# Row-wise infinity norm of an 8192 x 8192 matrix: another order and other cuts of the loads, a split first load, and a last result transposed before it is stored

## The chip, the core and the metric

The kernel runs on one core of one Trainium2 chip. The metric is the device time of one execution in microseconds. Most executions of one kernel agree within 0.3%. The profile shows a single execution and gives times from the start of its span.

## The reference

```python
def setup_inputs():
    return {
       "x": np.random.randn(8192, 8192).astype(np.float32),
    }

def reference(x: np.ndarray) -> np.ndarray:
    return np.linalg.norm(x, ord=np.inf, axis=1)
```

For a matrix given with `axis=1` this is the vector norm of each row: the largest absolute value among its 8192 elements. 8192 rows give 8192 results. The input is 268.4 MB of fp32, the output 32 KB; each element is read once and takes part in one maximum.

## The kernel before

A row of the matrix lies on one partition, so 128 rows of the matrix, one for each partition, make what this text calls a row of the tile grid, or simply a row: 128 partitions by 8192 columns, 4 MB. There are 64 such rows. They are numbered in 32 groups of R = 2 (L47, `x_g` in L53): partition p of group g holds the matrix rows 256 g + 2 p and 256 g + 2 p + 1, one after the other, 16384 columns. What one partition reads in a group is contiguous in HBM.

`_pieces` (L23) cuts this sequence of 64 x 8192 columns into loads. Up to where the tail begins each load is a whole group, 16384 columns. The tail is the list `TAIL` (L14): eight single rows of 8192 columns and then 14 pieces that shrink from 6400 to 1408. A piece that would cross a group's border is cut there. The list comes to 25 groups, 8 single rows and 14 pieces, 47 loads.

All loads go into one buffer, `ring` (L59), of three groups' size, 49,152 columns. A position `at` moves through it and returns to 0 when the next piece does not fit any more (L76). SP issues each load (L81), in order, and waits in front of it for the DVE reduces that read the columns which the load will overwrite. So at most three groups are in the ring, and a load is issued as soon as its part of the ring is free.

DVE takes each piece as it lands, in the same order. A whole row, or two, are reduced in one instruction straight into `res` (L87). A part of a row is reduced into a slot of `part` (L96), and when the row's last part is done a second reduce, the join, takes the maximum over its slots into `res` (L98). `absmax` (L65) is `tensor_reduce` with maximum and absolute value, on fp32.

`res` holds 64 results on each partition. When group 30 is complete, the results of the first 31 groups are transposed on TensorE into PSUM with an identity matrix (L108), copied by ACT to `o_sb` (L109) and stored from ACT's queue in two DMAs of 16 and 15 partitions, with 1 KB a partition (L111, L112). The last group's results, two numbers on each of 128 partitions, are stored directly by SP as 128 runs of 8 bytes (L113). This store waits for the last join.

There is no other order than that of the program on each engine: SP has the loads and the last store, DVE the reduces and joins, ACT the copies and two stores, TensorE two transposes, POOL the identity matrix at the start.

Of the kernel before, what the change touches and what calls it, by code (L numbers as in the profile page):

```python
# [1 line left out]

# [5 lines left out]

P = 128
FP32 = mybir.dt.float32  # L10

TAIL = (  # L14
    [8192] * 8
    + [6400, 5888, 4096]
    + [4992, 4544, 3776, 3072]
    + [3264, 2944, 2624, 2304, 2112, 1728, 1408]
)
RING = 3 * 16384  # L20


def _pieces(total, n_cols, pair):  # L23

    tail = sum(TAIL)
    assert (total - tail) % pair == 0
    cuts = [(a, a + pair) for a in range(0, total - tail, pair)]
    at = total - tail
    for w in TAIL:
        end = at + w  # L30
        while at < end:
            e = min(end, (at // pair + 1) * pair)
            cuts.append((at, e))
            at = e
    return cuts


@with_exitstack
def kernel(
    ctx: ExitStack,  # L40
    tc: tile.TileContext,
    x: bass.AP,
    out: bass.AP,
):
    nc = tc.nc
    n_rows, n_cols = x.shape
    R = 2  # L47
    pair = R * n_cols
    G = n_rows // (P * R)
    total = n_rows // P * n_cols  # L50


    x_g = x.rearrange("(g p r) m -> g p (r m)", p=P, r=R)  # L53
    out_g = out.rearrange("(g p r) -> g p r", p=P, r=R)

    single = ctx.enter_context(tc.tile_pool(name="single", bufs=1))
    psum_pool = ctx.enter_context(tc.tile_pool(name="psum", bufs=1, space=bass.MemoryType.PSUM))

    ring = single.tile([P, RING], FP32)  # L59
    res = single.tile([P, G, R], FP32)  # L60
    part = single.tile([P, G * R, 8], FP32)
    ident = single.tile([P, P], FP32)
    make_identity(nc, ident)

    def absmax(dst, src):  # L65
        nc.vector.tensor_reduce(  # L66
            out=dst, in_=src, axis=mybir.AxisListType.X,
            op=mybir.AluOpType.max, apply_absolute_value=True,
        )

    n_part = {}
    flushed = False
    at = 0
    for a, b in _pieces(total, n_cols, pair):
        w = b - a
        if at + w > RING:  # L76
            at = 0
        g = a // pair
        buf = ring[:, at : at + w]
        at += w  # L80
        nc.sync.dma_start(out=buf, in_=x_g[g, :, a - g * pair : b - g * pair])  # L81
        s = a
        while s < b:
            row = s // n_cols
            if s % n_cols == 0 and b - s >= n_cols:
                k = (b - s) // n_cols
                absmax(  # L87
                    res[:, g, row % R : row % R + k],
                    buf[:, s - a : s - a + k * n_cols].rearrange("p (k m) -> p k m", m=n_cols),
                )  # L90
                s += k * n_cols
                continue
            e = min(b, (row + 1) * n_cols)
            i = n_part.get(row, 0)
            n_part[row] = i + 1
            absmax(part[:, row, i : i + 1], buf[:, s - a : e - a])  # L96
            if e == (row + 1) * n_cols:
                nc.vector.tensor_reduce(  # L98
                    out=res[:, g, row % R : row % R + 1], in_=part[:, row, : i + 1],
                    axis=mybir.AxisListType.X, op=mybir.AluOpType.max,  # L100
                )
            s = e
        if b == (G - 1) * pair and not flushed:
            flushed = True
            o_sb = single.tile([G - 1, P, R], FP32)
            for r in range(R):
                o_ps = psum_pool.tile([G - 1, P], FP32, name=f"o_ps{r}")
                nc.tensor.transpose(o_ps, res[:, : G - 1, r], ident)  # L108
                nc.scalar.copy(o_sb[:, :, r], o_ps)  # L109
            h = (G - 1) // 2 + 1  # L110
            nc.scalar.dma_start(out=out_g[:h], in_=o_sb[:h])  # L111
            nc.scalar.dma_start(out=out_g[h : G - 1], in_=o_sb[h:])  # L112
    nc.sync.dma_start(out=out_g[G - 1], in_=res[:, G - 1, :])  # L113


# [1 line left out]
_INS = ['x']  # L117
_OUTS = [((8192,), 'float32')]


# [23 lines left out]
```

## Time and profile before

| | |
|---|---|
| median of 11 runs | 632.55 us (631.98 to 633.05) |
| the profiled execution | 632.35 us |
| its span | 630.5 us |
| DVE busy | 552.3 us, 88% of the span |
| HBM read | 268.44 MB, a mean of 426 GB/s over the span |
| first load issued, landed | 0.74 us, 22.54 us |
| last DVE wait for a load ends | 564.97 us |
| last join ends | 626.71 us |
| last store issued | 626.73 us, 2.8 us to landing |

The span is the time that the profile covers; the execution's own time is 1.85 us longer. The page divides the span into 40 slices and gives the busy share of each engine in tenths. The chain of waits is followed back from the last instruction: at each step to what released it, or to the instruction before it on the same engine. A time "to landing" counts from the issue of a DMA to its completion, so for loads that are issued early it contains the loads in front of them in the queue.

### The profile page before, as it was taken

To read this page: it belongs to the slowest core of one execution; us is meant where nothing else is said; L and a number is where in the kernel's file an instruction comes from. 1 tells how busy PE (TensorE), PEld (TensorE's weight loads), DVE (VectorE), ACT (ScalarE), POOL (GpSimd) and SP (SyncE) were. 2 spreads that over 40 slices of the span, in tenths; PEclk is the share of its full clock that TensorE was granted. 3 is DMA by queue.
4 is the path that set the end of the run, shared out by engine and by line. 5 is a ranking of instruction groups with operands and counts; after the bars stand their busy time and mean duration, and the time that the engine had idled before them with its cause. 6 is when DMAs were issued, how large, how long until landed. Compare 5 with 4: busy or idle time off the path is not lost.

```text
span 630.5 us, 200 instructions
## 1 busy us (share of the span) xinstructions
PE 0.8 (0%) x2; PEld 0.2 (0%) x2; DVE 552.3 (88%) x56; ACT 1.8 (0%) x3; POOL 0.7 (0%) x6
## 2 busy tenths in 40 slices
PE   0000000000000000000000000000000000000000
PEld 0000000000000000000000000000000000000000
DVE  0588988888988889888899888898888999999997
ACT  0000000000000000000000000000000000000000
POOL 0000000000000000000000000000000000000000
DMA  9999999999999999999999999999999999999995
GB/s 399 420 445 449 416 457 407 428 437 399 466 437 428 457 407 466 399 466 399 466 399 466 399 466 399 466 399 466 399 466 399 432 432 432 432 437 425 420 426 224
DMA packets 6975, 268.48 MB, mean 426 GB/s; under 512 B 927, under 2 KB 958, under 8 KB 1214
## 3 DMA queue, kind: packets, MB, share of 16 engines
q1 hardware_dynamic: 6912, 268.44, 98.8%
q10 hardware_dynamic: 62, 0.03, 0.0%
q14 instruction: 1, 0.01, 0.0%
HBM read 268.44 MB, written 0.03 MB: 426 GB/s over the span
## 4 chain that ended last, share of the span: by engine, by line
DMA 62%; DVE 37%; issue 0%
DMA ring<-in_x_dram 62%; DVE res L66 29%; DVE part L66 8%; DVE res L98 0%
## 5 line engine op out<-in xcount | busy, mean ns | idle before, releaser
L66 DVE TENSOR_REDUCE res<-ring 128x2 f32<-128x16384 f32 (+1 forms) x33 | 499.3, 15149 | 74.3 <-DMA ring<-in_x_dram 74.3
L66 DVE TENSOR_REDUCE part<-ring 128x1 f32<-128x4096 f32 (+15 forms) x17 | 52.7, 3156 | 0.0
L109 ACT COPY o_sb<-o_ps 31x128 f32<-31x128 f32 x2 | 0.5, 263 | 607.1 <-PE o_ps L108 607.1
L108 PE MATMUL o_ps<-ident,res 128*31 128x128 f32 x2 | 0.8, 404 | 608.5 <-DVE res L98 608.5
L109 ACT ACT_TABLE_LOAD x1 | 1.3, 1283 | 0.7 <-PEq L128 0.7
L98 DVE TENSOR_REDUCE res<-part 128x1 f32<-128x2 f32 (+2 forms) x6 | 0.9, 151 | 0.1
L108 PEld LDWEIGHTS o_ps<-ident,res 128*31 128x31 f32 x2 | 0.2, 125 | 608.8 <-issue 601.5
masks.py:199 POOL TENSOR_SCALAR_AFFINE_SELECT ident<-ident 128x128 f32<-128x128 f32 x1 | 0.3, 292 | 0.1
masks.py:197 POOL MEMSET ident<- 128x128 f32 x1 | 0.2, 204 | 0.3 <-POOLq L128 0.3
L128 POOL MEMSET const-bfloat16-1.0<- 128x1 bf16 x1 | 0.1, 101 | 0.0
L128 POOL MEMSET const-uint8-127<- 128x1 uint8 x1 | 0.1, 101 | 0.0
L128 POOL MEMSET const-float32-0.0<- 128x1 f32 x1 | 0.1, 98 | 0.2 <-issue 0.2
L128 POOL MEMSET const-float32-1.0<- 128x1 f32 x1 | 0.1, 98 | 0.0
## 6 DMA issues: line engine op xcount, KB each, us to landing
ring<-in_x_dram SPq DMA_DIRECT2D x8, 4096.0 KB, 40.5
ring<-in_x_dram SPq DMA_DIRECT2D x1, 3200.0 KB, 42.3
ring<-in_x_dram SPq DMA_DIRECT2D x1, 2944.0 KB, 40.7
ring<-in_x_dram SPq DMA_DIRECT2D x1, 2496.0 KB, 42.9
ring<-in_x_dram SPq DMA_DIRECT2D x1, 2272.0 KB, 39.7
ring<-in_x_dram SPq DMA_DIRECT2D x1, 2048.0 KB, 45.2
ring<-in_x_dram SPq DMA_DIRECT2D x1, 1888.0 KB, 44.0
ring<-in_x_dram SPq DMA_DIRECT2D x1, 1632.0 KB, 43.4
```

The source lines that it names most:

```text
L66: nc.vector.tensor_reduce(out=dst, in_=src, axis=mybir.AxisListType.X, op=mybir.AluOpType.max, apply_absolute_value=True,)
L98: nc.vector.tensor_reduce(out=res[:, g, row % R : row % R + 1], in_=part[:, row, : i + 1], axis=mybir.AxisListType.X, op=mybir.AluOpType.max,)
L108: nc.tensor.transpose(o_ps, res[:, : G - 1, r], ident)
L109: nc.scalar.copy(o_sb[:, :, r], o_ps)
L128: nc = _bacc.Bacc("TRN2", target_bir_lowering=False, num_devices=1)
```

## The change

The order and the cuts of the loads are written out in `PIECES`: four single rows first, then 24 pairs as whole loads, four pairs that are cut (into 2, 2, 2 and 3 pieces), three single rows cut into 2, 3 and 4 pieces, and the last row in six pieces from 1792 down to 896. The single rows have the matrix's last 1024 rows, one matrix row on each partition; the pairs have the others, two on each partition as before.

The first load is issued as two DMAs, partitions 0 to 15 and partitions 16 to 127.

Rows from number `CUT` = 48 on go into `part`, which has K = 4 slots for each and is cleared by POOL at the start. One reduce over all slots of 15 rows replaces the joins. It stands after the last but one row, and the stores of the first 63 rows' results follow it: `pairs_out` (two transposes, one store of 28 partitions) and `singles_out` (one transpose, one store of 7 partitions), on TensorE, ACT and ACT's queue.

The last row's first five pieces leave their maxima in five columns behind the buffer of its sixth piece, `last`, which lies outside the ring. The final reduce covers the sixth piece and these columns at once. Its result, one number on each of 128 partitions, is transposed on TensorE, copied from PSUM by DVE and stored by SP from one partition, 512 bytes.

```diff
--- before.py
+++ after.py
@@ -8,31 +8,25 @@
 
 P = 128
 FP32 = mybir.dt.float32
+MAX = mybir.AluOpType.max
 
 
 
-TAIL = (
-    [8192] * 8
-    + [6400, 5888, 4096]
-    + [4992, 4544, 3776, 3072]
-    + [3264, 2944, 2624, 2304, 2112, 1728, 1408]
+
+HEAD = 4
+PAIRS = 28
+PIECES = (
+    [[8192]] * HEAD
+    + [[16384]] * 24
+    + [[7232, 9152], [6720, 9664], [8640, 7744], [5568, 5568, 5248]]
+    + [[4480, 3712], [3392, 1920, 2880], [2752, 1600, 2048, 1792]]
+    + [[1792, 1664, 1472, 1280, 1088, 896]]
 )
 RING = 3 * 16384
 
 
-def _pieces(total, n_cols, pair):
-
-    tail = sum(TAIL)
-    assert (total - tail) % pair == 0
-    cuts = [(a, a + pair) for a in range(0, total - tail, pair)]
-    at = total - tail
-    for w in TAIL:
-        end = at + w
-        while at < end:
-            e = min(end, (at // pair + 1) * pair)
-            cuts.append((at, e))
-            at = e
-    return cuts
+CUT = 48
+K = 4
 
 
 @with_exitstack
@@ -44,73 +38,114 @@
 ):
     nc = tc.nc
     n_rows, n_cols = x.shape
-    R = 2
-    pair = R * n_cols
-    G = n_rows // (P * R)
-    total = n_rows // P * n_cols
+    R = n_rows // P
+    assert R == 64 and n_cols == 8192
 
-
-    x_g = x.rearrange("(g p r) m -> g p (r m)", p=P, r=R)
-    out_g = out.rearrange("(g p r) -> g p r", p=P, r=R)
+    X_ONE = 2 * PAIRS
 
     single = ctx.enter_context(tc.tile_pool(name="single", bufs=1))
     psum_pool = ctx.enter_context(tc.tile_pool(name="psum", bufs=1, space=bass.MemoryType.PSUM))
 
     ring = single.tile([P, RING], FP32)
-    res = single.tile([P, G, R], FP32)
-    part = single.tile([P, G * R, 8], FP32)
+    res = single.tile([P, R - 1], FP32)
+    part = single.tile([P, R - 1 - CUT, K], FP32)
+    nc.gpsimd.memset(part, 0.0)
     ident = single.tile([P, P], FP32)
     make_identity(nc, ident)
 
+
+    n_last = len(PIECES[-1]) - 1
+    w_last = PIECES[-1][-1]
+    last = single.tile([P, w_last + n_last], FP32)
+    fin = single.tile([P, 1], FP32)
+
     def absmax(dst, src):
         nc.vector.tensor_reduce(
-            out=dst, in_=src, axis=mybir.AxisListType.X,
-            op=mybir.AluOpType.max, apply_absolute_value=True,
+            out=dst, in_=src, axis=mybir.AxisListType.X, op=MAX, apply_absolute_value=True,
         )
 
-    n_part = {}
-    flushed = False
+    def singles_out():
+        n = R - 1 - X_ONE
+        ps = psum_pool.tile([n, P], FP32, name="ps_singles")
+        sb = single.tile([n, P], FP32, name="sb_singles")
+        nc.tensor.transpose(ps, res[:, X_ONE:], ident)
+        nc.scalar.copy(sb, ps)
+        nc.scalar.dma_start(
+            out=out[X_ONE * P : (R - 1) * P].rearrange("(r p) -> r p", p=P), in_=sb
+        )
+
+    def pairs_out():
+        sb = single.tile([PAIRS, P, 2], FP32, name="sb_pairs")
+        both = res[:, :X_ONE].rearrange("p (g r) -> p g r", r=2)
+        for r in range(2):
+            ps = psum_pool.tile([PAIRS, P], FP32, name=f"ps_pairs{r}")
+            nc.tensor.transpose(ps, both[:, :, r], ident)
+            nc.scalar.copy(sb[:, :, r], ps)
+        nc.scalar.dma_start(
+            out=out[: X_ONE * P].rearrange("(g p r) -> g p r", p=P, r=2), in_=sb
+        )
+
     at = 0
-    for a, b in _pieces(total, n_cols, pair):
-        w = b - a
-        if at + w > RING:
-            at = 0
-        g = a // pair
-        buf = ring[:, at : at + w]
-        at += w
-        nc.sync.dma_start(out=buf, in_=x_g[g, :, a - g * pair : b - g * pair])
-        s = a
-        while s < b:
-            row = s // n_cols
-            if s % n_cols == 0 and b - s >= n_cols:
-                k = (b - s) // n_cols
-                absmax(
-                    res[:, g, row % R : row % R + k],
-                    buf[:, s - a : s - a + k * n_cols].rearrange("p (k m) -> p k m", m=n_cols),
-                )
-                s += k * n_cols
-                continue
-            e = min(b, (row + 1) * n_cols)
-            i = n_part.get(row, 0)
-            n_part[row] = i + 1
-            absmax(part[:, row, i : i + 1], buf[:, s - a : e - a])
-            if e == (row + 1) * n_cols:
-                nc.vector.tensor_reduce(
-                    out=res[:, g, row % R : row % R + 1], in_=part[:, row, : i + 1],
-                    axis=mybir.AxisListType.X, op=mybir.AluOpType.max,
-                )
-            s = e
-        if b == (G - 1) * pair and not flushed:
-            flushed = True
-            o_sb = single.tile([G - 1, P, R], FP32)
-            for r in range(R):
-                o_ps = psum_pool.tile([G - 1, P], FP32, name=f"o_ps{r}")
-                nc.tensor.transpose(o_ps, res[:, : G - 1, r], ident)
-                nc.scalar.copy(o_sb[:, :, r], o_ps)
-            h = (G - 1) // 2 + 1
-            nc.scalar.dma_start(out=out_g[:h], in_=o_sb[:h])
-            nc.scalar.dma_start(out=out_g[h : G - 1], in_=o_sb[h:])
-    nc.sync.dma_start(out=out_g[G - 1], in_=res[:, G - 1, :])
+    next_pair, next_one = 0, X_ONE
+    for u, widths in enumerate(PIECES):
+        k = sum(widths) // n_cols
+        if k == 2:
+            row, next_pair = next_pair, next_pair + 2
+        else:
+            row, next_one = next_one, next_one + 1
+        src = x[row * P : (row + k) * P].rearrange("(p r) m -> p (r m)", r=k)
+        off = 0
+        n_part = {}
+        for h, w in enumerate(widths):
+            final = u == len(PIECES) - 1 and h == n_last
+            if final:
+                buf = last[:, :w]
+            else:
+                if at + w > RING:
+                    at = 0
+                buf = ring[:, at : at + w]
+                at += w
+            if u == 0:
+                nc.sync.dma_start(out=buf[:16], in_=src[:16, off : off + w])
+                nc.sync.dma_start(out=buf[16:], in_=src[16:, off : off + w])
+            else:
+                nc.sync.dma_start(out=buf, in_=src[:, off : off + w])
+            if final:
+                absmax(fin[:, :1], last)
+                break
+            s = 0
+            while s < w:
+                r = row + (off + s) // n_cols
+                left = n_cols - (off + s) % n_cols
+                c = (w - s) // n_cols if left == n_cols else 0
+                if c and r + c <= CUT:
+                    absmax(
+                        res[:, r : r + c],
+                        buf[:, s : s + c * n_cols].rearrange("p (c m) -> p c m", m=n_cols),
+                    )
+                    s += c * n_cols
+                    continue
+                e = min(w, s + left)
+                i = n_part.get(r, 0)
+                n_part[r] = i + 1
+                if r == R - 1:
+                    absmax(last[:, w_last + i : w_last + i + 1], buf[:, s:e])
+                else:
+                    absmax(part[:, r - CUT, i : i + 1], buf[:, s:e])
+                s = e
+            off += w
+        if u == len(PIECES) - 2:
+            nc.vector.tensor_reduce(
+                out=res[:, CUT:], in_=part, axis=mybir.AxisListType.X, op=MAX,
+            )
+            pairs_out()
+            singles_out()
+
+    fin_ps = psum_pool.tile([1, P], FP32)
+    fin_sb = single.tile([1, P], FP32)
+    nc.tensor.transpose(fin_ps, fin, ident)
+    nc.vector.tensor_copy(out=fin_sb, in_=fin_ps)
+    nc.sync.dma_start(out=out[(R - 1) * P :].rearrange("(r p) -> r p", p=P), in_=fin_sb)
 
 
 # ---- launch: one core; inputs and outputs as the reference has them ----
```

## The prediction, made before the changed kernel had run

> **What bounds the kernel now.** I read the page's shares and 40 slices first, then the chain of waits, then the groups split by shape, the windows of the start, the timeline of the tail and the DMA issues.
>
> ```profile
> PE 0.8 (0%) x2; PEld 0.2 (0%) x2; DVE 552.3 (88%) x56; ACT 1.8 (0%) x3; POOL 0.7 (0%) x6
> DVE  0588988888988889888899888898888999999997
> DMA  9999999999999999999999999999999999999995
> ```
>
> The DMA engines are full from the first slice to the last but one, DVE is near 88% and reaches 9 only in the last ten slices. So the load stream is the bound for most of the span and DVE comes close to it. The chain of waits shows where one hands over to the other:
>
> ```profile
> 0.74 21.80 DMA ring<-in_x_dram
> ...
> 446.49 40.78 DMA ring<-in_x_dram
> 487.27 0.02 issue
> 487.29 34.42 DVE res L66 x3
> 521.71 0.02 issue
> 521.73 43.24 DMA ring<-in_x_dram
> 564.97 0.02 issue
> 564.99 8.69 DVE res L66
> ...
> 618.41 8.12 DVE part L66 x4
> 626.52 0.02 issue
> 626.55 0.16 DVE res L98
> ```
>
> Columns are start, duration, what. Up to 487.27 each step is a load, and 50 of the 64 column rows (a row is 8192 columns on each partition) have landed. The eight single rows that follow land 9.71 us apart ((564.97 - 487.27) / 8). The last wait of DVE for a load ends at 564.97. From there DVE runs without a gap to 626.71: the end is set by DVE, not by the last landing.
>
> ```profile
> L66 DVE TENSOR_REDUCE res<-ring 128x2 f32<-128x16384 f32 x25 | 430.5, 17220 | 74.0 <-DMA ring<-in_x_dram 74.0
> L66 DVE TENSOR_REDUCE res<-ring 128x1 f32<-128x8192 f32 x8 | 68.9, 8677 | 0.3 <-DMA ring<-in_x_dram 0.3
> L66 DVE TENSOR_REDUCE part<-ring 128x1 f32<-128x1408 f32 x1 | 1.6, 1610 | 0.0
> ```
>
> 17220 minus 8677 over 8192 columns is 1.043 ns a column, and what is left is about 0.14 us an instruction, part of which overlaps the instruction before. In the gapless stretch 564.99 to 626.71 there are 57,344 columns in 24 instructions (18 reduces, 6 joins): at 1.0417 ns a column (the slope from 16384 down to 1408 columns) 59.73 us are columns, so 1.99 us, 83 ns for each instruction, are overhead. A load costs 1.18 ns a column (19.35 us between starts of two pair reduces, over 16384). DVE thus gains only 0.14 ns a column on the stream, while at a pair's landing it is 17.22 us behind.
>
> ```profile
> 0.00:22.56 22.56, 0.00 (x0) 0.00 (x0) 0.00 (x0) 1.28 (x1) 0.70 (x6) 1.00 1.00 418
> 22.56:41.91 19.35, 0.00 (x0) 0.00 (x0) 17.22 (x1) 0.00 (x0) 0.00 (x0) 1.00 1.00 434
> ```
>
> The last column of the windows is GB/s. The first pair takes 21.80 us from issue where 19.35 is the steady figure: 2.45 us of start, of which 0.98 us pass before the first packet in the trace's packet records.
>
> ```profile
> 608.90 0.42 PE L108 MATMUL o_ps<-ident,res 128*31 128x128 f32 x1 [6.96 <-DVE res L98]
> 609.36 0.26 ACT L109 COPY o_sb<-o_ps 31x128 f32<-31x128 f32 x1 [7.12 <-PE o_ps L108]
> 609.65 0.38 ACTq L111 DMA_DIRECT2D out_dram<-o_sb  x1
> 626.73 0.35 SPq L113 DMA_DIRECT2D out_dram<-res  x1
> ```
>
> The final store is issued 0.02 us after the last join and lands 2.79 us later (2.8 in the list of issues), at 629.52; the span ends 0.98 us after that. The transpose at 608.90 is the model for the new one.
>
> [...] In the packet records the 8-byte store lands 1.75 us after its last packet, the 1 KB-row stores 0.48 us after theirs[...].
>
> **The change part by part.** The diff is priced as it stands: the last row is transposed on TensorE and stored as one 512 byte run, not on DVE in 128 byte runs as the words of the change have it.
>
> *Order and cuts of the rows.* Four single rows, then 24 pairs, then 12 rows in 24 pieces. SP issues without a stall: the ring still holds 49,152 columns, a slot comes free 17.2 us after its landing, and then 19.35 plus 2.13 us of loads are still queued. In the tail the pieces are small and the ring holds over ten of them. Starting with single rows lets DVE begin some 9.7 us earlier, which is worth nothing, as DVE then waits for loads anyway (2.13 us before each pair, 74.0 in all).
> The tail is worth something. Before, the last pair lands with 14 rows to go, now with 12. Before, 52 rows had landed at 487.27 + 2 x 9.71 = 506.70. Two more singles in place of a pair cost 2 x 0.04 us and the first tile's second DMA about as little: 506.8. From there DVE has the pair, 17.22 us, then 98,304 columns, 102.40 us, in 28 reduces (four pieces cross a row's end) and one join, 29 x 0.083 = 2.41 us; the join over 60 elements and the 5 old partials in the final reduce add 0.06. DVE ends at 506.83 + 17.22 + 102.40 + 2.41 + 0.06 = 628.92, against 626.71: **+2.21 us**. The stream would deliver the last piece near 624.5 (before: 624.33), so DVE is some 3 to 4 us behind it all along the tail, and no piece's landing is waited for. Six joins merged into one and the last row's join folded into its last reduce are in this count.
>
> *The last row's result.* New after the last reduce: semaphore to TensorE 0.04 and transpose 0.42 (row at 608.90), 0.04 to the copy, a copy of 1 x 128 out of PSUM on DVE, then 0.02 to SP. The copy is not in the trace; ACT's is 0.26[...]. Sum 0.78, less the 0.02 of before: **+0.76 us**. Nothing hides it; DVE has nothing else to do.
>
> *The final store.* One 512 byte run in place of 128 of 8 bytes. Upper bound: 2.79 as before. Lower bound: 0.85 to the first packet (626.73 to 627.58), 0.05 of data, 0.48 to landing, 1.38 us. I take 1.6, nearer the lower[...]: **-1.2 us**.
>
> *The other stores* (28 rows of 1 KB, 7 of 512 B) go out on ACT's queue once the merged join is done, about 619.4. Two transposes, copies and an issue, then 5 us to landing under load as before, 626 to 627: hidden behind the last row's reduces. If that cover went, the late part would be 1 or 2 us. The memset of the partials on POOL is done long before the first landing: nothing.
>
> *The first tile in two DMAs.* SP issues once more, 0.33 us, while the queue is full: nothing. [...] The start's own delay (about 1.1 us of 2.45 lie after the first packet) can hide inside it, some 0.7. [...] A tile lands with its slowest engine, and the stream never gets a loss back, since it is full. Bounds -0.3 us [...] and +8.5. I take 3.64 - 0.7 + 1.3 = **+4.2 us**. All of it moves the landing of row 52 and DVE's chain with it.
>
> Sum against the profiled execution: 630.5 + 2.21 + 0.76 - 1.2 + 4.2 = 636.5 span. That execution took 632.35, 1.85 more than its span: 638.3. It lies 0.2 below the median, 632.55, so 638.5.
>
> **The rivals.**
> [...] (first tile costs nothing): 630.5 + 2.21 + 0.76 - 1.2 = 632.3, with 2.05 added 634.3, 0.3% slower. For it: the two DMAs follow each other in one queue and engines might run ahead into the second. [...]
> *Not slower, the start is won.* [...] Price: up to 0.25 us of the 0.98 and 0.7 to 0.8 of the 1.1, near -1.0. [...] that gives 633.3, with the store at its lower bound 633.1, within 0.2% of before. It decides from a start that lands row 52 at 506.1 or sooner. For it: 2.45 us of start are visible. Against: the time to the first packet of the tiny last store is 0.85, hardly less than 0.98.
> *The split is worse than priced*: [...] 8.5 us of start, 642.8.
>
> **How the numbers follow.** [...] as priced 0.50 (about 636.8 to 640.5), worse than priced 0.12[...], start won 0.12. The range leaves out the start won and most of the worst case: 633.5 to 642. A run of this kernel can tell a change from none at about 0.2%, 1.27 us (631.3 to 633.8). Slower: 0.50 + 0.12 + three quarters of 0.26 and a little of the last, 0.83; same 0.13; faster 0.04.
>
> **What would show it.** Right: the last DVE wait for a load ends at the last full pair, and DVE is gapless from there for 122 us; the last piece lands 3 us or more before its reduce starts; the first single lands near 16 us[...]; a PE, a DVE copy and a store shorter than 2 us end the chain. Wrong: DVE waiting for pieces in the tail (then the lag was mis-sized), a first landing below 13 us [...], or a final store again near 2.8 us. The forecast falls as a whole if the first landing and every later one stand where they did; what is left then is the 0.3% of the tail.

## The result: 1.5% slower

The changed kernel takes 641.99 us in the median (641.83 to 642.27, 8 runs), against 632.49 for the kernel before in the same comparison (31 runs). The ratio is 1.0151, with a 95% interval of 1.0142 to 1.0160. The forecast was 638.5 with a range of 633.5 to 642.0: the direction held, and the loss, 9.5 us, was 1.6 times the forecast one, at the very edge of the range.

First the rates, from the page (HBM rate in 40 slices of about 16 us, the kernel before and then the changed one) and from the windows of the changed kernel (the last column is GB/s):

```profile
GB/s 399 420 445 449 416 457 407 428 437 399 466 437 428 457 407 466 399 466 399 466 399 466 399 466 399 466 399 466 399 466 399 432 432 432 432 437 425 420 426 224
GB/s 203 375 434 430 454 418 438 450 401 458 442 409 454 401 454 450 401 458 426 426 454 397 458 450 401 454 413 442 450 401 458 442 394 439 435 427 425 421 422 202
```
```profile
0.00:22.60 22.60, 0.00 (x0) 0.00 (x0) 0.00 (x0) 1.28 (x1) 0.78 (x7) 1.00 0.95 229
22.60:32.20 9.60, 0.00 (x0) 0.00 (x0) 8.69 (x1) 0.00 (x0) 0.00 (x0) 1.00 1.02 437
```

The first slice moves half of what it did before, the second is lower too, the third and later ones run as before. The first tile, 4 MB, lands at 22.60 us, when the kernel before had 8 MB: 229 GB/s in place of 418. Note the next to last column, the share of time in which the DMA engines had a packet: 0.95. They are occupied nearly all the while and move at about half the rate, so the busy share of the DMA engines does not show the loss. From the second tile on (437 GB/s) the rate is as it was.

The chain of waits of the changed kernel (start, duration, what):

```profile
475.23 40.78 DMA ring<-in_x_dram
516.01 0.03 issue
516.04 17.22 DVE res L63
533.26 95.19 DVE part L63 x22
628.45 0.02 issue
628.48 0.22 DVE res L138
...
636.62 1.10 DVE fin L63
637.73 0.04 issue
637.77 0.39 PE fin_ps L146
638.15 0.02 issue
638.18 0.28 DVE fin_sb L147
```

The end of the first line is the landing of row 52, at 516.01. The kernel before had it at 506.70 (487.27 plus two rows of 9.71), so 9.31 us are lost by then. From there DVE is without a pause to the end of the final reduce, 637.71, as the forecast had it: 121.70 us, against 120.01 in the kernel before (506.70 to 626.71), 1.69 more. The end in the timeline of the changed kernel (start, duration, engine, line):

```profile
636.62 1.09 DVE L63 TENSOR_REDUCE fin<-last 128x1 f32<-128x901 f32 x1
637.77 0.37 PE L146 MATMUL fin_ps<-ident,fin 128*1 128x128 f32 x1 [8.13 <-DVE fin L63]
638.18 0.28 DVE L147 COPY fin_sb<-fin_ps 1x128 f32<-1x128 f32 x1 [0.46 <-PE fin_ps L146]
638.48 0.31 SPq L148 DMA_DIRECT2D out_dram<-fin_sb  x1
```

The store is issued 0.77 us after the end of the final reduce (637.71), before it was 0.02: 0.75 more. From its issue to the end of the span, 640.4, are 1.92 us, before 3.77 (626.73 to 630.5): 1.85 less. The four terms, 9.31 + 1.69 + 0.75 - 1.85, make 9.90, the difference of the spans (640.4 and 630.5).

### The profile page after: what moved, and what is told of

The parts are those of the page before. It is cut to its first block, busy times and chain, and to the rows that moved or that the text cites. A ratio compares the mean times of both kernels' runs of the same rounds, so it can differ in the third digit from the quotient of the medians.

```text
span 640.4 us, 217 instructions
## 1 busy us (share of the span) xinstructions
PE 1.2 (0%) x4; PEld 0.4 (0%) x4; DVE 552.7 (86%) x58; ACT 2.0 (0%) x4; POOL 0.8 (0%) x7
## 4 chain that ended last, share of the span: by engine, by line
DMA 60%; DVE 39%; SPq 0%; issue 0%; PE 0%
DMA ring<-in_x_dram 60%; DVE res L63 22%; DVE part L63 16%; DVE last L63 1%; DVE fin L63 0%; SPq L112 0%; SPq L110 0%; PE fin_ps L146 0%; SPq L109 0%; DVE fin_sb L147 0%; DVE res L138 0%
## 5 line engine op out<-in xcount | busy, mean ns | idle before, releaser
L63 DVE TENSOR_REDUCE res<-ring 128x2 f32<-128x16384 f32 x24 | 413.3, 17220 | 59.7 <-DMA ring<-in_x_dram 59.7
L63 DVE TENSOR_REDUCE part<-ring 128x1 f32<-128x8192 f32 (+19 forms) x26 | 130.0, 5066 | 25.6 <-DMA ring<-in_x_dram 25.6
L63 DVE TENSOR_REDUCE last<-ring 128x1 f32<-128x1792 f32 (+4 forms) x5 | 8.0, 1662 | 0.0
```

What stands on the lines that cost most here:

```text
L63: nc.vector.tensor_reduce(out=dst, in_=src, axis=mybir.AxisListType.X, op=MAX, apply_absolute_value=True,)
```

## The experiments

**The split undone.**

```diff
-            if u == 0:
-                nc.sync.dma_start(out=buf[:16], in_=src[:16, off : off + w])
-                nc.sync.dma_start(out=buf[16:], in_=src[16:, off : off + w])
-            else:
-                nc.sync.dma_start(out=buf, in_=src[:, off : off + w])
+            nc.sync.dma_start(out=buf, in_=src[:, off : off + w])
```

> The changed kernel with its first tile in one load of 128 partitions. Theory 1, the split carries the whole loss at the start: first tile lands near 12.6 us, row 52 near 506.8, the chain from there 121.7 as in the changed kernel, so 633.0 us, within 0.2% of before. Rival, the order (single rows first) or the many small pieces carry part of the loss: row 52 still later than 508 us and the time above 635 us.

Measured: 632.77 us, ratio to the kernel before 1.0005 (0.9996 to 1.0014), no change that can be told. The DVE timeline of this kernel, and two lines of its chain:

```profile
13.03 8.69 DVE L63 TENSOR_REDUCE part<-ring 128x1 f32<-128x8192 f32 x1 [13.03 <-DMA ring<-in_x_dram]
22.65 8.69 DVE L63 TENSOR_REDUCE part<-ring 128x1 f32<-128x8192 f32 x1 [0.93 <-DMA ring<-in_x_dram]
32.34 8.69 DVE L63 TENSOR_REDUCE part<-ring 128x1 f32<-128x8192 f32 x1 [1.01 <-DMA ring<-in_x_dram]
42.06 8.69 DVE L63 TENSOR_REDUCE part<-ring 128x1 f32<-128x8192 f32 x1 [1.03 <-DMA ring<-in_x_dram]
```
```profile
506.46 0.02 issue
506.49 17.22 DVE res L63
```

Each DVE start here is the landing of a row. The first is at 13.03, 9.57 us sooner than with the split, and row 52 at 506.46, 9.55 sooner. The loss is whole at the first landing and nothing is added or won back after it. The split carries all of it. Order, cuts and new ending together change nothing measurable, because they offset each other: DVE takes the same 121.70 us from row 52 on as in the changed kernel, 1.69 more than before, and the ending takes about 1.0 less than before.

**The split elsewhere, and on longer rows.** In one kernel `if u == 0` became `if u == 3`, which splits the fourth row. In the other the kernel before got the split on its first load, 64 KB a partition:

```diff
-        nc.sync.dma_start(out=buf, in_=x_g[g, :, a - g * pair : b - g * pair])
+        src = x_g[g, :, a - g * pair : b - g * pair]
+        if a == 0:
+            nc.sync.dma_start(out=buf[:16], in_=src[:16])
+            nc.sync.dma_start(out=buf[16:], in_=src[16:])
+        else:
+            nc.sync.dma_start(out=buf, in_=src)
```

> The changed kernel with the split on the fourth tile in place of the first. Theory 1, [...]: the first tile lands near 12.6 us, the fourth near 51.5 (41.8 plus 9.7), row 52 at 516 to 517, time 642. Rival, the loss is a matter of the cold start: row 52 near 507, time 633.

> The kernel before with only the split of its first load, whose rows are 64 KB, twice as long. Theory 1, the loss goes with the bytes: twice 9.2 to 9.9 us, first pair lands near 41 to 42 us, time 651 to 652. Rival, a fixed price of a second DMA or of few rows: 9 to 10 us as in the changed kernel, first pair near 32 us, time 642.

Measured in one run each: 643.19 and 654.31 us, beside 632.47 for the kernel before. The DVE timeline of the first, then of the second:

```profile
33.49 8.69 DVE L63 TENSOR_REDUCE part<-ring 128x1 f32<-128x8192 f32 x1 [2.10 <-DMA ring<-in_x_dram]
52.83 8.69 DVE L63 TENSOR_REDUCE part<-ring 128x1 f32<-128x8192 f32 x1 [10.65 <-DMA ring<-in_x_dram]
```
```profile
44.81 17.22 DVE L66 TENSOR_REDUCE res<-ring 128x2 f32<-128x16384 f32 x1 [44.81 <-DMA ring<-in_x_dram]
```

The fourth row lands at 52.83 in place of 42.06, 10.8 us late, in mid stream. The third is already 1.15 late (33.49 against 32.34). The trace's packet records, which have the start, duration and size of each DMA packet, show its last packets ending as without the split (32.0 us in both kernels): only its completion comes later. With 64 KB rows the first pair lands 22.25 us late (44.81 against 22.56), 2.3 times the loss for twice the bytes, and about 3 us later than expected. So it is not a matter of the start, nor a fixed price for a second DMA. In mid stream the split is dearer by 1.2 us than at the start; that a part of the start hides in the loss, as the forecast had it, agrees with this and is not shown by it.

**Which of the two loads.** One full first load, with an additional load ahead of it, once of the 16 and once of the 112 partitions, into a part of the ring that is free then:

```diff
+            if u == 0:
+                nc.sync.dma_start(out=ring[0:16, 40960:49152], in_=src[0:16, :])
             nc.sync.dma_start(out=buf, in_=src[:, off : off + w])
```

> One full first load, with an additional load of partitions 0 to 15 (32 KB each) ahead of it whose data nobody reads. Theory 1, [...]: 4.1 to 4.9 us more, first tile lands at 16.7 to 17.5 us, row 52 near 511. Rival, sixteen rows cost only their bytes, 1.2 us, and the loss of the changed kernel is in the 112 rows: first tile near 13.8 us, row 52 near 508.

> One full first load, with an additional load of partitions 16 to 127 ahead of it whose data nobody reads. If the 112 rows lose nothing: 8.5 us more than 12.6, first tile near 21.1 us. The forecast's model [...]: 8.5 to 10.9, first tile 21.1 to 23.5 us. If the changed kernel's loss is mostly theirs: 14 to 15 us more, first tile 26.5 to 28 us, row 52 near 521.

Measured in one run each: 636.75 and 648.06 us. First landings, with 16 and then with 112 additional partitions:

```profile
17.13 8.69 DVE L63 TENSOR_REDUCE part<-ring 128x1 f32<-128x8192 f32 x1 [17.13 <-DMA ring<-in_x_dram]
```
```profile
28.44 8.69 DVE L63 TENSOR_REDUCE part<-ring 128x1 f32<-128x8192 f32 x1 [28.44 <-DMA ring<-in_x_dram]
```

Against 13.03 without them: 4.10 us for the 16 rows and 15.41 for the 112. A row of 32 KB takes an engine 1.21 us (9.71 / 8; the median of the 1,024 packets of 32 KB in the packet records of the kernel before is 1.218), so at full rate these are 1.21 and 8.5 us. The 16 rows lose 2.9 us, the 112 lose 6.9. Together 9.8, which fits the 9.57 of the changed kernel. The changed kernel's own packet records agree. Its two loads show 16 and 112 packets of 32 KB and 16 completions each, so one row and seven rows to each of the 16 engines; from the median start of its first sixteen packets, the 16 rows, to that of the next sixteen are 3.7 us (1.9 without the split), and the seven packets of the 112 rows take 14.95 us (8.5 without the split). Most of the loss is where the forecast had placed the lesser part of it.

**Other halves.** The split as partitions 0 to 63 and 64 to 127, then as even and odd partitions. The edit of the second:

```diff
-                nc.sync.dma_start(out=buf[:16], in_=src[:16, off : off + w])
-                nc.sync.dma_start(out=buf[16:], in_=src[16:, off : off + w])
+                nc.sync.dma_start(out=buf[0:128:2], in_=src[0:128:2, off : off + w])
+                nc.sync.dma_start(out=buf[1:128:2], in_=src[1:128:2, off : off + w])
```

> The changed kernel with the first tile split as partitions 0 to 63 and 64 to 127. Theory 1, [...] a row takes 2.43 us: 9.7 us lost, first tile near 22.3 us, row 52 near 516.5. Rival, the loss comes from the sixteen row piece or from a row count that is no power of two: first tile near 12.7 us, row 52 near 506.9.

> The changed kernel with the first tile split as even and odd partitions, 64 rows each. [...] nothing is lost: first tile near 12.7 us. If it is decided by which rows an engine gets [...]: 9.7 us lost, first tile near 22.3 us.

Measured in one run each: 643.27 and 632.98 us. First landings, halves and then even and odd:

```profile
23.68 8.69 DVE L63 TENSOR_REDUCE part<-ring 128x1 f32<-128x8192 f32 x1 [23.68 <-DMA ring<-in_x_dram]
```
```profile
13.33 8.69 DVE L63 TENSOR_REDUCE part<-ring 128x1 f32<-128x8192 f32 x1 [13.33 <-DMA ring<-in_x_dram]
```

Two loads with the same count of rows, the same bytes and the same order cost 10.65 us or at most 0.30 us, by which partitions they reach. The 0.30 is hardly more than the spread: with one full first load the first landing lay between 13.03 and 13.25 us in four kernels. In the packet records a row of 32 KB takes about 2.55 us in the halves and 1.21 in the even and odd ones. This rules out the number of DMAs and the number of rows as the cause: 64 neighbours got about 206 GB/s (2.10 MB as 4 rows on each of 16 engines, in 4 x 2.55 us), 64 partitions two apart about 433 (in 4 x 1.21 us).

On which side of the transfer the time is lost is not shown. In all these runs partition p of a load takes the p-th run of its rows in HBM, so neighbouring partitions also read neighbouring memory. A load of every second matrix row into neighbouring partitions would tell the two apart; it was not run.

**Other sets.** Additional loads of 16 KB a partition that nobody reads stand ahead of the second, third and fourth row, with the split undone:

```diff
+            if 1 <= u <= 3:
+                rows = (slice(0, 16), slice(0, 128, 8), slice(16, 128))[u - 1]
+                lo = 32768 + 4096 * u
+                nc.sync.dma_start(out=ring[rows, lo : lo + 4096], in_=src[rows, :4096])
             nc.sync.dma_start(out=buf, in_=src[:, off : off + w])
```

> One full first load; between the four single rows, three additional loads with 16 KB a partition that nobody reads: partitions 0 to 15 ahead of the second row, every eighth partition (16 in all) ahead of the third, 16 to 127 ahead of the fourth. The gap between the landings of two rows is 9.6 to 9.7 us without them. Theory, [...] 2.4 more in the first gap [...], 1.2 in the second [...], and 7.7 in the third if the 112 rows lose in mid stream what they lost at the start. Rival for the second, the count of partitions decides: 2.4 as in the first.

> As the kernel with three additional loads, with partitions 0 to 111 ahead of the second row, 32 to 127 ahead of the third and 0 to 31 ahead of the fourth. If 112 rows lose because of how they are dealt to the engines, wherever they begin: 7.7 us more in the first gap. 96 rows, six to an engine: 3.6 if nothing is lost, up to 6.1 [...], 6.6 if a row costs what it does among 112. 32 rows [...]: 2.4 us more in the third gap, 1.2 if nothing is lost.

Measured in one run each: 645.16 and 649.66 us. The DVE timelines, the first kernel and then the second:

```profile
14.20 8.69 DVE L63 TENSOR_REDUCE part<-ring 128x1 f32<-128x8192 f32 x1 [14.20 <-DMA ring<-in_x_dram]
26.36 8.69 DVE L63 TENSOR_REDUCE part<-ring 128x1 f32<-128x8192 f32 x1 [3.48 <-DMA ring<-in_x_dram]
37.70 8.69 DVE L63 TENSOR_REDUCE part<-ring 128x1 f32<-128x8192 f32 x1 [2.66 <-DMA ring<-in_x_dram]
54.43 8.69 DVE L63 TENSOR_REDUCE part<-ring 128x1 f32<-128x8192 f32 x1 [8.04 <-DMA ring<-in_x_dram]
```
```profile
13.47 8.69 DVE L63 TENSOR_REDUCE part<-ring 128x1 f32<-128x8192 f32 x1 [13.47 <-DMA ring<-in_x_dram]
30.22 8.69 DVE L63 TENSOR_REDUCE part<-ring 128x1 f32<-128x8192 f32 x1 [8.06 <-DMA ring<-in_x_dram]
46.93 8.69 DVE L63 TENSOR_REDUCE part<-ring 128x1 f32<-128x8192 f32 x1 [8.03 <-DMA ring<-in_x_dram]
58.92 8.69 DVE L63 TENSOR_REDUCE part<-ring 128x1 f32<-128x8192 f32 x1 [3.30 <-DMA ring<-in_x_dram]
```

A gap between two landings, less the 9.62, 9.69 and 9.72 without additional loads, gives 2.54, 1.65 and 7.01 us in the first kernel, 7.13, 7.02 and 2.27 in the second. A load also holds up the row ahead of it by up to 1.2 us, so a gap is known to about 1 us. In the packet records the median packet of the row behind the additional load starts later by 2.8, 1.7 and 7.4 us, and by 6.5, 7.3 and 2.9. At full rate the bytes need 0.6 us for 16 rows, 1.2 for 32, 3.6 for 96 and 4.2 for 112.

Sixteen rows over all partitions cost about 1 us less than sixteen neighbours, no more than the gaps are sure to; with the halves it agrees that the count does not decide. They are not free either: 1.7 us, where 1.2 was expected and their bytes alone take 0.6. The 112 rows lose in mid stream what they lost at the start (about 3 us with half the bytes) and nearly as much from partition 0 on. The 96 rows cost as much as the 112, at or above the highest of the three values expected, 6.6. Seven rows to an engine are thus not special. Why 96 or 112 neighbours lose so much was not found. The expectations rested on an assumption of the author, shown in no trace, of how much neighbours delay each other. Its values come near for the 16 rows (2.4 us expected, 2.5 measured), the 32 (2.4 and 2.3) and the halves (9.7 and 10.65), but it gave at most 6.1 us for the 96 and 10.9 for the 112 rows of 32 KB, where 7.0 and 15.4 were measured. If the rows that an engine gets decided, 9.7 us would have been lost for the even and odd sets, where at most 0.3 were.

**The lag of DVE.** In the kernel without the split, three of the four single rows were moved behind the pairs:

```diff
-HEAD = 4
+HEAD = 1
...
     + [[16384]] * 24
+    + [[8192]] * 3
```

> One full first load, one single row at the head, and three of the four single rows moved behind the 24 pairs, so that 15 rows and not 12 follow the last pair. Theory, DVE's lag behind the loads is what the new tail costs: DVE catches up, the final reduce ends near 625.6 to 626.0 us in place of 628.5, time 630.1 to 630.6 us, 0.3 to 0.4% faster than before. Rival, the lag is hidden or comes from the small pieces: 633 us as with four at the head.

Measured: 630.92 us (11 runs), ratio to the kernel before 0.9976 (0.9967 to 0.9985), 0.24% faster than before and 0.3% faster than with four singles at the head. The end of its chain:

```profile
512.41 33.53 DMA ring<-in_x_dram
545.94 0.02 issue
545.97 71.17 DVE part L64 x18
617.14 0.02 issue
617.17 0.22 DVE res L135
617.38 7.91 DVE last L64 x5
625.29 0.02 issue
625.31 1.10 DVE fin L64
```

DVE waits for a load once more at 545.94, and its final reduce ends at 626.41, against 628.16 with four singles at the head. That is 1.75 us; the expected end, 625.6 to 626.0, was missed by 0.4 us and the time by 0.3. The last load lands 0.3 us before its reduce starts (624.99 in the trace's completion records), so the lag is nearly gone. Against the kernel before, the final reduce ends 0.30 us sooner than the last join did (626.71), and the ending takes about 1.0 us less.

**The last store.** Without the split, the last row's results go out from 128 partitions:

```diff
-    nc.tensor.transpose(fin_ps, fin, ident)
-    nc.vector.tensor_copy(out=fin_sb, in_=fin_ps)
-    nc.sync.dma_start(out=out[(R - 1) * P :].rearrange("(r p) -> r p", p=P), in_=fin_sb)
+    nc.sync.dma_start(out=out[(R - 1) * P :].rearrange("(p r) -> p r", r=1), in_=fin)
```

> One full first load, and the last row's 128 results stored straight from 128 partitions in runs of 4 bytes, without the transpose and the copy. Theory, the transpose's 0.76 us are more than paid by a shorter store: 0.76 less before the issue, 2.79 in place of 1.1 us to landing, 0.9 us slower than the one with the transpose. Rival, the store's length is not a matter of its runs: 0.76 us faster.

Measured: 638.60 us (5 runs), ratio to the kernel before 1.0099 (1.0084 to 1.0113), 5.8 us slower than with the transpose. The timeline's line, then that of the issues (the last column is the time to landing):

```profile
628.45 0.35 SPq L140 DMA_DIRECT2D out_dram<-fin  x1
```
```profile
out_dram<-fin SPq DMA_DIRECT2D x1, 0.5 KB, 7.1
```

The expected direction was right and the size, 0.9 us, was missed by a factor of more than six: 128 runs of 4 bytes take 7.1 us to land, where 128 runs of 8 bytes took 2.8 in the kernel before.

## Why the prediction was too low

- **The split, "the first tile in two DMAs".** This is the step that failed, by its size: +4.2 us forecast, +9.3 measured at row 52; the first single was to land near 16 us and landed at 22.60. That the loss would arise at the first tile and be kept to the end held: 9.57 us at its landing and 9.55 at row 52, against the kernel without the split. The forecast took 3.64 us for the 16 rows, less 0.7 for the start, and 1.3 for the 112. All loads of the kernel before reach 128 partitions, so its trace shows neither loss; both were the author's assumptions. The term for the 16 rows held: 2.94 us, and 2.9 measured with the additional load. The term that was mis-sized is that of the 112 rows: it measures 6.9 us with the additional load, and 6.5 for the median packet in the changed kernel itself. In the runs a row of 16 or 32 KB among 96 or 112 neighbours takes about 1.5 to 2 times as long as one among 128 (14.95 us in place of 8.5 for seven rows of 32 KB in the changed kernel); why stays open. The upper bound, +8.5, did not hold the value either.
- **The tail.** DVE's lag was called the bound of the tail, and DVE ran without a pause from row 52 on. Forecast +2.21 us, of which 0.13 lie before row 52 lands; from there +1.69 measured where 2.08 were forecast. The error is the 83 ns of overhead for each instruction: 121.70 - 17.22 - 102.40 - 0.06 leaves 2.0 us for 29, 70 ns. The 83 ns were a mean over 24 instructions, three of them joins that waited for the reduce just before; from reduce to reduce both traces have 60 ns. The last piece landed 2.9 us before its reduce (633.73 in the completion records), where 3 or more were named as a sign. The kernel with the singles behind the pairs supports the lag as the cause: it took 1.75 us off the end.
- **The transpose.** Forecast +0.76, measured +0.75. DVE's copy took 0.28 us; the forecast's sum has 0.26 for it, the time of ACT's copy in the trace of before.
- **The store.** Forecast -1.2, measured -1.85 at the end of the span. The lower bound, 1.38 from issue to landing, was still too long. The trace shows 1.1: 0.74 to the packet, 0.03 of data and 0.34 to landing. That one long run lands sooner was right; whether the length of the runs or their number decides, the changed kernel does not tell apart.
- **The other stores** were hidden behind the last row: issued at 629.76 and 630.46 and, in the completion records, done by 633.73, before the final reduce at 636.62.
- **The rivals.** The rival in which the first tile costs nothing (a chance of 0.26) and the one in which the start is won fell with the first landing at 22.60. That the small DMA gets the stream moving sooner is not seen: the first packet is at 1.74 us in the packet records, 1.72 before. "The split is worse than priced" was the closest, at a chance of 0.12; its 642.8 is 0.8 us above the result.
- **Slips that changed nothing.** DVE shows a 9 in six slices ahead of the last ten too. The chain up to 487.27 is not loads alone; a pair's reduce of 17.23 us stands between every two stretches of 40.8 us of loads. The slope from 16384 to 1408 columns is 1.042 ns; 1.0417 is that between 6400 and 640. The 12.6 us for a first single without loss should have been 12.9 by the forecast's own terms (0.74 + 2.45 + 9.71); 13.03 was measured.

Without the split the sum would have been 634.3; the kernel without it measured 632.77. The tail (0.4 us), the store (0.65) and the landing of row 52 (506.46 where 506.83 was forecast) make up nearly all of this 1.5 us. So the split was 5.1 us too cheap and the rest 1.5 us too dear, and it was luck that the total came out only 3.5 us low.

## What to carry to other kernels

In a kernel bound by its loads, keep every load on all 128 partitions, and cut a tile by columns if it must be cut; here 16 and 112 neighbours in place of 128 cost 9.6 us for a 4 MB tile, and the DMA engines had a packet 0.95 of the time, whereas the tail's pieces, cut by columns, still came in at 421 to 439 GB/s. If partitions are divided, take every second one: in the one run of it here that cost at most 0.3 us. At the end of a load-bound kernel, count how many columns follow the last large piece, since a reducer that is only 13% faster than the loads (1.04 against 1.18 ns a column) needs them all to catch up. And put the last few results on one partition before they are stored: here that cost 0.75 us and saved 1.85.

## What the runs showed that had not been expected

Ninety-six neighbouring partitions (32 to 127) are no better than 112: with 16 KB each they took about 7 us, twice the 3.6 us of their bytes. And the time of a store in tiny runs is not set by its bytes or its count of runs alone: 128 runs of 4 bytes into 512 bytes took 7.1 us, 128 runs of 8 bytes into 1 KB 2.8 us, one run of 512 bytes 1.1 us. Why the store with runs half as long takes two and a half times as long was not tried.
